# Block sums of the first MLP matrix, formed by adding transfers on GpSimd's queue instead of by VectorE

## The chip, the cores and the metric

The kernel runs on one core of a Trainium2 chip. The metric is device time in microseconds, from launch to end. Of the kernel before there are two timed runs, 1002.09 and 1002.58 us (median 1002.34), and one further execution that was profiled. Engines go by their profile names: PE (TensorE, with its weight loads shown as PEld), DVE (VectorE), ACT (ScalarE), POOL (GpSimd) and SP (SyncE, which here only issues transfers).

## The reference, cut to what matters

One layer of a hybrid decoder on 512 prompt tokens and 64 new tokens (576 columns in all). Two branches (RWKV-7 and attention) are merged to `m`; what the change touches is what follows:

```python
x = x + m @ lp['w_out']
hn = rmsnorm(x, lp['g_ffn'], NORM_EPS)
x = x + jnp.square(jax.nn.relu(hn @ lp['w_up'])) @ lp['w_down']
```

`w_out` is 1024 x 1024, `w_up` 1024 x 4096, `w_down` 4096 x 1024, all float32.

## The kernel before, in words

Everything is held transposed: channels on the 128 partitions, tokens in the free dimension. Every float32 operand of a large product is split in two: ACT copies it to a rounded `hi`, DVE subtracts to get `lo`, and PE multiplies hi·hi, hi·lo and lo·hi. So each weight tile that is loaded costs one ACT and one DVE instruction ("halving") before PE can use it.

**The output projection** (`dense(w_out[d], ...)`, called wo0, wo4, wo1, wo5, wo2, wo6, wo3, wo7 in this order) has 48 matmuls for each of its eight output tiles: two column halves of 288, 8 inner tiles, 3 products. Its weights come as two tiles of 4 inner blocks each (`raw_wo5_0` and `raw_wo5_4`, halved to `hi_wo5_0`/`lo_wo5_0` and `hi_wo5_1`/`lo_wo5_1`). Its result is taken from PSUM by DVE (`ya`, line 61), scaled on ACT to `hf`, and made at once into the seven blocks of the next product's moving operand (`h_b11`, `h_t1` and so on, by `put`).

**The first MLP matrix** is done with a seven-product scheme on 2 x 2 blocks in place of eight products. `up_pair(f1)` takes a pair of 128-row output tiles f1 and f1+1: the stationary blocks are a11, a12 (tile f1, first and second half of the inner dimension) and a21, a22 (tile f1+1). DVE forms four block sums of 128 x 512: s12 holds a21+a22 and a21+a22-a11, s34 holds a11-a21 and a12-(a21+a22-a11). Then s12, the tile of a11 and a12, s34 and a22 are halved, and seven products of 12 matmuls each run on PE in the order S1 (`uc`), A11 (`ua`), S2 (`ub`), A12 (`ua`), S3 (`ux`), S4 (`ud`), A22 (`ux`). There are 16 pairs. After a pair, four output tiles of the second matrix (`down`, `ps_dn`, 96 matmuls) run, except in the first and the last group of two pairs.

**Order.** A scheduler fixes each engine's order at build time from priorities (`prio`): loads of a job go first, halvings next, matmuls fill. On the chip every engine runs its row strictly in that order, and an instruction whose semaphore has not come stops all behind it on that engine, the transfer queues of SP and POOL included. Buffers are rings: `a` (the loaded rows of `w_up`) has 3 tiles of 512 KB, `s` 2, the halves `hi2`/`lo2` 3 each, and the ring of the other weights (`raw`, 256 KB) 3.

Of the kernel before, what the change touches and what calls it, by code (L numbers as in the profile page):

```python
# [8 lines left out]
F32 = mybir.dt.float32  # L9
F32R = mybir.dt.float32r  # L10
I32 = mybir.dt.int32
AF = mybir.ActivationFunctionType
# [3 lines left out]
P = 128  # L16
# [25 lines left out]
def tile_hybrid_step(ctx, tc, xT, xsT, ktab, vtab, s0T, ptab, w_in, vecs, w2a2, g2, lamv,  # L42
                     w_bra, w_brb, w_out, w_up, w_down, cst, bias_p, bias_s,
                     yT, kTo, vTo, Sp, Ss, sh):
    nc = tc.nc
# [9 lines left out]
    ring = {"job": 0}  # L55

    def act(out, in_, func=AF.Copy, **kw):
        ring["act"] = AE.activation(out=out, in_=in_, func=func, **kw)  # L58

    def tt(out, a, b, op, eng=None):  # L60
        ins = (eng or VE).tensor_tensor(out=out, in0=a, in1=b, op=op)  # L61
        if eng is None:
            ring["tt"] = ins

    def stt(out, a, s, b, op0, op1):
        VE.scalar_tensor_tensor(out=out, in0=a, scalar=s, in1=b, op0=op0, op1=op1)
# [16 lines left out]
    FEED, LATE, FILL = -1000000, 500000, 1000000  # L83

    @contextmanager
    def prio(at):
        was, tc.cur_priority = tc.cur_priority, at
        yield
        tc.cur_priority = was

    MUL, ADD, SUB, MAX = ALU.mult, ALU.add, ALU.subtract, ALU.max
# [20 lines left out]
    c = const.tile([P, C_END], F32, name="cst_sb")  # L112
# [158 lines left out]
    with tc.tile_pool(name="xin", bufs=2, reuse_waits="tile") as xin:  # L271
# [6 lines left out]
        for k in range(0, KT, 4):  # L278
            for j in range(3):
                with prio(FEED + 1000 + 10 * k + j):  # L280
                    name = f"raw_{'qkv'[j]}0_{k}"
                    if k == 0:
                        raw = ring["pool"].tile([P, 4, P], F32, tag="raw", name=name, bufs=3)
                    else:
                        raw = zw.tile([P, 1 + NX], F32, tag="z" if j else "tz", name=name,
                                      bufs=2 if j else 1)[:, :4 * P].rearrange("p (k w) -> p k w", k=4)
# [378 lines left out]
    for h in range(HB):  # L665
        if h:
            qkv(h)
        for cc in range(2):
            GE.tensor_copy(
                out=qbd[64 * cc:64 * cc + 64, :, h, 8 * cc:8 * cc + 8],  # L670
                in_=qT[64 * cc:64 * cc + 64, h, NPR:].rearrange("p (b q) -> p b q", b=NB))
# [448 lines left out]
    sp_ = pool("sp", 4, stack=ctx, reuse_waits="tile")  # L1120
# [6 lines left out]
    hfs = {}  # L1127
    for i, d in enumerate((0, 4, 1, 5, 2, 6, 3, 7)):
        xr = wt_.tile([P, NT], F32, tag="xr", name=f"xr{d}")
        with prio(FEED + 1000 * (ring["job"] + 1) - 1):  # L1130
            nc.sync.dma_start(out=xr, in_=xT[:, d])
        hf = hfs[d] = wt_.tile([P, NT], F32, tag="hf", name=f"hf{d}", bufs=3)
        k = d % 4

        def ev(ps, t0, n, d=d, k=k, xr=xr, hf=hf):
            x, h = ya[:, d, t0:t0 + n], hf[:, t0:t0 + n]
            tt(x, ps, xr[:, t0:t0 + n], ADD)
            act(h, x, scale=v(V_GF + d))
            if d < 4:
                if t0 == 0:  # L1140
                    put("b11", k, h)
                else:
                    t1 = wt_.tile([P, 288], F32, tag="t", name=f"t1_{k}", bufs=4)
                    tt(t1, h, hf[:, :288], SUB)
                    hfs["t1", k] = t1
                    put("t1", k, t1)
            elif t0:
                for n, x, y in (("t2", h, hfs["t1", k]), ("t3", h, hfs[k][:, 288:])):
                    t = hfs[n] = wt_.tile([P, 288], F32, tag="t", name=f"{n}_{k}", bufs=4)
                    tt(t, x, y, SUB)  # L1150
                    put(n, k, t)
                put("b22", k, h)
            else:
                put("b21", k, h)
                t4 = wt_.tile([P, 288], F32, tag="t", name=f"t4_{k}", bufs=4)
                tt(t4, h, hfs["t2"], SUB)
                put("t4", k, t4)
        dense(w_out[d], KT, mh, ml, HALF[::1 if d < 4 else -1], ev, f"wo{d}")

        for j, (t0, n) in enumerate(HALF):  # L1160
            o = acc[:, t0:t0 + n]
            if i == 0:
                act(o, ya[:, d, t0:t0 + n], AF.Square)
            else:
                sq = cbank(j, f"sq{d}{j}")[:, :n]
                act(sq, ya[:, d, t0:t0 + n], AF.Square)
                tt(o, o, sq, ADD)
# [12 lines left out]
    def up_pair(f1):  # L1180

        f2 = f1 + 1
        for f in (f1, f2):
            qs[f] = hq_pool.tile([P, 2, NT], F32R, tag="q", name=f"q{f}")
        with prio(FEED + 1000 * (ring["job"] + 1)):
            rows = [sp_.tile([P, 2, 4, P], F32, tag="raw", name=f"a{f}", bufs=3) for f in (f1, f2)]
            for r, f in zip(rows, (f1, f2)):
                nc.sync.dma_start(out=r.rearrange("p i k w -> p (i k) w"), in_=w_up[f])
        (a11, a12), (a21, a22) = ([r[:, i] for i in range(2)] for r in rows)
        s12, s34 = (sp_.tile([P, 2, 4, P], F32, tag="s", name=f"s{i}_{f1}", bufs=2) for i in (12, 34))  # L1190

        def halve(x, two, after):

            pl = sp_ if two else ring["pool"]
            shape = [P, 2, 4, P] if two else [P, 4, P]
            hi, lo = (pl.tile(shape, F32R, tag=t + "2" * two, name=f"{t}{after}_{f1}", bufs=3)
                      for t in ("hi", "lo"))
            with prio(FEED + 1000 * (ring["job"] + after) + 100):
                act(hi, x)
                tt(lo, x, f32(hi), SUB)  # L1200
            return [(hi[:, i], lo[:, i]) for i in range(2)] if two else (hi, lo)

        with prio(FEED + 1000 * (ring["job"] + 1) + 90):
            tt(s12[:, 0], a21, a22, ADD)
            tt(s12[:, 1], s12[:, 0], a11, SUB)
        S1, S2 = halve(s12, True, 1)
        A11, A12 = halve(rows[0], True, 2)
        with prio(FEED + 1000 * (ring["job"] + 3) + 90):
            tt(s34[:, 0], a11, a21, SUB)
            tt(s34[:, 1], a12, s12[:, 1], SUB)  # L1210
        S3, S4 = halve(s34, True, 5)
        A22 = halve(a22, False, 7)

        def e(n):
            return ft.tile([P, LAST[0][1]], F32, tag=n[0], name=f"{n}_{f1}", bufs=4 if n[0] == "c" else 1)[:, :288]

        def product(lhs, blk, ps, start, stop):
            job = ring["job"] = ring["job"] + 1
            i = 0
            skip = not (start and stop)  # L1220
            for k in range(4):
                for l, h in ((lhs[0], 0), (lhs[0], 1), (lhs[1], 0)):
                    with prio(FILL + 1000 * job + i):
                        ring["mm"] = PE.matmul(out=ps[:, :288], lhsT=l[:, k], rhs=hb[blk][:, h, k],  # L1224
                                               start=start and i == 0, stop=i == 11,
                                               skip_group_check=skip)
                    i += 1
            return prio(FEED + 1000 * job + 200)

        def out(f, half, c, r=None):  # L1230

            sp = slice(288 * half, 288 * half + 288)
            r = c if r is None else r
            act(r, c, AF.Relu)
            act(r, r, AF.Square)
            act(qs[f][:, 0, sp], r)
            tt(qs[f][:, 1, sp], r, f32(qs[f][:, 0, sp]), SUB)

        ba, bb, bc_, bx = (cbank(0, f"ua{f1}"), cbank(1, f"ub{f1}"), tbank(f"uc{f1}"), bank(f"ux{f1}"))
        product(S1, "t1", bc_, True, True)  # L1240
        with product(A11, "b11", ba, True, False):
            p1 = e("p1")
            act(p1, ba[:, :288])
        with product(S2, "t2", bb, True, True):
            u = e("u")
            tt(u, bb[:, :288], p1, ADD)
            w = e("w")
            tt(w, bc_[:, :288], u, ADD)
        with product(A12, "b21", ba, False, True):
            out(f1, 0, ba[:, :288], e("c11"))  # L1250
        with product(S3, "t3", bx, True, False):
            c22 = e("c22")
            tt(c22, bx[:, :288], w, ADD)
            out(f2, 1, c22)
        bd = cbank(1, f"ud{f1}")
        with product(S4, "b22", bd, True, True):
            c12 = e("c12")
            tt(c12, bd[:, :288], w, ADD)
            out(f1, 1, c12)
        with product(A22, "t4", bx, False, True):  # L1260
            c21 = e("c21")
            tt(c21, bx[:, :288], u, ADD)
            out(f2, 0, c21)
        ahead.append((ring["act"], ring["tt"]))
# [15 lines left out]
    for ch in range(8):  # L1280
        for i in range(2):
            up_pair(4 * ch + 2 * i)
            if ch == 0 and i == 0:
# [4 lines left out]
                with prio(FEED + 1000 * ring["job"]):  # L1288
                    m2 = stat.tile([P, 5], F32, tag="r", name="m2")
                    r2 = stat.tile([P, 5], F32, tag="s", name="r2")  # L1290
# [13 lines left out]
    rows = []  # L1304
    for d, n in enumerate((None, "t1", "b11", "t2", "b21", "t3", "b22", "t4")):
        if n:
            t = fp.tile([P, 2, 4, 288], F32R, tag=f"h_{n}", name=f"w3_{d}", bufs=1)
            t = t.rearrange("p i k t -> p (i k t)")
# [6 lines left out]
    for t0, n in LAST:  # L1315
# [55 lines left out]
        w = slice(0, len(tiles))  # L1371
# [133 lines left out]
```

## Time and profile before

| what | value |
|---|---|
| timed runs | 1002.09 and 1002.58 us, median 1002.34 |
| profiled execution, span from first to last instruction | 1004.0 us |
| PE busy | 975.5 us (97%) |
| DVE, ACT, POOL busy | 689.5, 497.3, 88.3 us |
| moved by DMA | 105.75 MB, mean 105 GB/s |

The profile gives the profiled execution's span and no other time of it; the span lies 1.7 us above the median of the timed runs, which were taken without the profiler. The page shows busy time by engine, the span in 40 slices, transfers by queue, the chain of work that ended last, and groups of instructions. Line numbers in its rows are those of the kernel before; line 58 is the helper for ACT, lines 61 and 66 those for two-input DVE instructions, line 72 the matmul helper, 1188 the loads of `w_up`, 1224 the matmuls of the seven products.

### The profile page before, as it was taken

The numbers are of one execution on the slowest core, as the hardware profiler recorded it, in microseconds if no ns is written. First come the engines' busy times: TensorE is split into PE (matmuls) and PEld (weight loads), VectorE is DVE, ScalarE is ACT, GpSimd is POOL, SyncE is SP. The second block draws the span as 40 slices with busy tenths as digits, with TensorE's granted clock in tenths as the row PEclk, the third lists the DMA queues.
The fourth block names the chain that finished last, engine by engine and source line by source line (L and its number), as shares of the span: only waits on it lengthen the run. The fifth ranks groups of instructions, "written<-read, shape, count | busy, mean of one in ns | idle before, by whom it ended". The sixth has DMA issues, their size and how long they took to land.

```text
span 1004.0 us, 24422 instructions
## 1 busy us (share of the span) xinstructions
PE 975.5 (97%) x10012; PEld 919.9 (92%) x10012; DVE 689.5 (69%) x1459; ACT 497.3 (50%) x1094; POOL 88.3 (9%) x171
## 2 busy tenths in 40 slices
PE   8999999899999999999999999999999999999996
PEld 8999998898887878888889999999999999999996
DVE  6698666774946669445588798966666666666744
ACT  6576555354435344443344666644444444444732
POOL 2511001301010340000300000000000000000001
PEclk9999999999989989999999999999999999999998
DMA  7312673121111225222377642222222222221402
GB/s 265 142 66 88 204 221 120 54 64 45 43 47 57 69 87 171 80 70 102 106 215 237 195 152 74 95 85 95 85 85 95 84 85 85 85 84 44 128 10 95
DMA packets 50833, 105.75 MB, mean 105 GB/s; under 512 B 6066, under 2 KB 8114, under 8 KB 50594
## 3 DMA queue, kind: packets, MB, share of 16 engines
q1 hardware_dynamic: 47442, 96.95, 30.2%
q0 software_dynamic: 1648, 5.35, 1.4%
q8 instruction: 79, 1.29, 0.5%
q10 hardware_dynamic: 1632, 1.89, 0.5%
q14 instruction: 32, 0.26, 0.1%
HBM read 89.38 MB, written 14.78 MB: 104 GB/s over the span
## 4 chain that ended last, share of the span: by engine, by line
PE 86%; DVE 6%; ACT 3%; DMA 2%; issue 2%; POOL 1%; SPq 0%; DVEq 0%; POOLq 0%; ACTq 0%
PE ps_dn L72 21%; PE ps_g L72 9%; PE ps_z L72 8%; PE ua L1224 5%; PE ux L1224 5%; PE ps_wo L72 4%; PE uc L1224 3%; PE ud L1224 3%; PE ub L1224 3%; PE ps_k L72 2%; PE ps_brb L72 2%; PE pch L72 2%; PE ps_q L72 2%; PE ps_v L72 2%; PE pA L72 2%
## 5 line engine op out<-in xcount | busy, mean ns | idle before, releaser
L72 PE MATMUL ps_dn<-q,hi_dn 128*128 128x288 f32 x768 | 154.7, 296 | 0.0
L72 PEld LDWEIGHTS ps_dn<-q,hi_dn 128*128 128x128 f32 x768 | 122.8, 188 | 1.5
L72 PE MATMUL ps_dn<-q,lo_dn 128*128 128x288 f32 x384 | 113.2, 295 | 0.0
L72 PE MATMUL ps_g<-xl,hi_g 128*128 128x288 f32 x256 | 80.2, 313 | 0.0
L72 PE MATMUL ps_g<-xh,lo_g 128*128 128x288 f32 x256 | 79.3, 310 | 0.0
L72 PE MATMUL ps_g<-xh,hi_g 128*128 128x288 f32 x256 | 79.2, 310 | 0.0
L72 PEld LDWEIGHTS ps_dn<-q,lo_dn 128*128 128x128 f32 x384 | 72.1, 188 | 0.0
L72 PE MATMUL ps_z<-xh,lo_z 128*128 128x288 f32 (+1 forms) x224 | 69.6, 311 | 0.0
L72 PE MATMUL ps_z<-xh,hi_z 128*128 128x288 f32 (+1 forms) x224 | 68.3, 305 | 0.0
L72 PE MATMUL ps_z<-xl,hi_z 128*128 128x288 f32 (+1 forms) x224 | 67.6, 302 | 0.0
L61 DVE TENSOR_TENSOR ya<-ya,ps_dn 128x288 f32<-128x288 f32 x96 | 43.4, 453 | 29.3 <-PE ps_dn L72 29.3
L58 ACT ACTIVATE hi_dn<-raw_dn 128x512 fp32r<-128x512 f32 x48 | 30.1, 628 | 57.0 <-PE ps_dn L72 57.0
L1224 PE MATMUL ua<-h_b,hi 128*128 128x288 f32 x256 | 53.2, 298 | 0.0
L1224 PE MATMUL ux<-h_t,hi 128*128 128x288 f32 x256 | 52.3, 296 | 0.0
L58 ACT ACTIVATE c<-c 128x288 f32<-128x288 f32 x112 | 48.4, 439 | 7.5 <-DVE c L61 5.8
L72 PEld LDWEIGHTS ps_g<-xh,hi_g 128*128 128x128 f32 x256 | 49.0, 191 | 2.9 <-issue 1.6
L72 PEld LDWEIGHTS ps_g<-xl,hi_g 128*128 128x128 f32 x256 | 49.0, 191 | 1.9
L72 PEld LDWEIGHTS ps_g<-xh,lo_g 128*128 128x128 f32 x256 | 49.1, 192 | 1.4
L58 ACT ACTIVATE hi<-a 128x1024 fp32r<-128x1024 f32 (+1 forms) x32 | 27.1, 846 | 42.0 <-PE ps_dn L72 34.3
L72 PE MATMUL ps_dn<-q,w 128*128 128x320 f32 (+1 forms) x336 | 46.4, 298 | 0.0
L61 DVE TENSOR_TENSOR lo<-s,hi 128x1024 fp32r<-128x1024 f32 x32 | 39.2, 1225 | 10.2 <-ACT hi L58 10.0
L72 PEld LDWEIGHTS ps_dn<-q,w 128*128 128x128 f32 x336 | 45.3, 190 | 0.1
(395 smaller groups left out, 2801.7 us busy)
## 6 DMA issues: line engine op xcount, KB each, us to landing
a<-in_w_up_dram SPq DMA_DIRECT2D x32, 512.0 KB, 3.3
raw_dn<-in_w_down_dram SPq DMA_DIRECT2D x64, 256.0 KB, 2.9
raw_g<-in_w_in_dram SPq DMA_DIRECT2D x32, 256.0 KB, 3.2
raw_z<-in_w_in_dram SPq DMA_DIRECT2D x28, 256.0 KB, 3.0
gt_d<-gg SPq DMA_DIRECT2D x16, 288.0 KB, 2.5
g<-gt_d SPq DMA_DIRECT2D x16, 288.0 KB, 3.7
kp<-in_ktab_dram SPq DMA_DIRECT2D x16, 256.0 KB, 4.0
vp<-in_vtab_dram SPq DMA_DIRECT2D x16, 256.0 KB, 3.7
```

What stands on the lines that cost most here:

```text
L58: ring["act"] = AE.activation(out=out, in_=in_, func=func, **kw)
L61: ins = (eng or VE).tensor_tensor(out=out, in0=a, in1=b, op=op)
L72: ring["mm"] = PE.matmul(out=out, lhsT=lhsT, rhs=rhs, start=start, stop=stop)
L1224: ring["mm"] = PE.matmul(out=ps[:, :288], lhsT=l[:, k], rhs=hb[blk][:, h, k], start=start and i == 0, stop=i == 11, skip_group_check=skip)
```

## The change

The second row tile of each pair enters with its sign turned, so that all four block sums are plain sums: s12 holds a21+a22 and a11+a21+a22, s34 holds a11+a21 and a12+a11+a21+a22. The signs are made good in three of the moving blocks (t1, t2 and t4 are formed negated, t2 and t4 by a `scalar_tensor_tensor`, one instruction as before) and in the Relu of the second tile, whose scale is -1.

The sums are no longer made by DVE. SP loads one addend into each half of the s tile (plain transfers), and POOL's queue then issues transfers from DRAM that add onto what lies in SBUF (`accum_op=ADD`): two for s12, three for s34. a1 and a22 are loaded by themselves. The ring of s12, a1 and s34 has 5 tiles of 512 KB; a22 comes from the 3-tile ring that the second matrix's weights use.

```diff
                     t1 = wt_.tile([P, 288], F32, tag="t", name=f"t1_{k}", bufs=4)
-                    tt(t1, h, hf[:, :288], SUB)
+                    tt(t1, hf[:, :288], h, SUB)
...
-                for n, x, y in (("t2", h, hfs["t1", k]), ("t3", h, hfs[k][:, 288:])):
+                for n in ("t2", "t3"):
                     t = hfs[n] = wt_.tile([P, 288], F32, tag="t", name=f"{n}_{k}", bufs=4)
-                    tt(t, x, y, SUB)
+                    if n == "t2":
+                        stt(t, h, -1.0, hfs["t1", k], MUL, SUB)
+                    else:
+                        tt(t, h, hfs[k][:, 288:], SUB)
...
-                tt(t4, h, hfs["t2"], SUB)
+                stt(t4, hfs["t2"], -1.0, h, MUL, SUB)
...
-            rows = [sp_.tile([P, 2, 4, P], F32, tag="raw", name=f"a{f}", bufs=3) for f in (f1, f2)]
-            for r, f in zip(rows, (f1, f2)):
-                nc.sync.dma_start(out=r.rearrange("p i k w -> p (i k) w"), in_=w_up[f])
-        (a11, a12), (a21, a22) = ([r[:, i] for i in range(2)] for r in rows)
-        s12, s34 = (sp_.tile([P, 2, 4, P], F32, tag="s", name=f"s{i}_{f1}", bufs=2) for i in (12, 34))
+            s12, a1, s34 = (sp_.tile([P, 2, 4, P], F32, tag="raw", name=f"{n}{f1}", bufs=5)
+                            for n in ("s12", "a1", "s34"))
+            a22 = ring["pool"].tile([P, 4, P], F32, tag="raw", name=f"a22{f1}", bufs=3)
+            r1, r2 = (w_up[f].rearrange("p (i k) w -> p i (k w)", i=2) for f in (f1, f2))
+            flat = lambda t: t.rearrange("p i k w -> p i (k w)")
+            twice = lambda r, i: r[:, i:i + 1].broadcast_to([P, 2, 4 * P])
+            nc.sync.dma_start(out=flat(s12)[:, 0], in_=r2[:, 0])
+            nc.sync.dma_start(out=flat(s12)[:, 1], in_=r1[:, 0])
+            nc.gpsimd.dma_start(out=flat(s12), in_=twice(r2, 1), accum_op=ADD)
+            nc.gpsimd.dma_start(out=flat(s12)[:, 1], in_=r2[:, 0], accum_op=ADD)
+            nc.sync.dma_start(out=flat(a1), in_=r1)
+            nc.sync.dma_start(out=flat(s34)[:, 0], in_=r2[:, 0])
+            nc.sync.dma_start(out=flat(s34)[:, 1], in_=r1[:, 1])
+            nc.gpsimd.dma_start(out=flat(s34), in_=twice(r1, 0), accum_op=ADD)
+            nc.gpsimd.dma_start(out=flat(s34)[:, 1:2], in_=r2[:, 0:1], accum_op=ADD)
+            nc.gpsimd.dma_start(out=flat(s34)[:, 1:2], in_=r2[:, 1:2], accum_op=ADD)
+            nc.sync.dma_start(out=a22.rearrange("p k w -> p (k w)"), in_=r2[:, 1])
...
-        with prio(FEED + 1000 * (ring["job"] + 1) + 90):
-            tt(s12[:, 0], a21, a22, ADD)
-            tt(s12[:, 1], s12[:, 0], a11, SUB)
         S1, S2 = halve(s12, True, 1)
-        A11, A12 = halve(rows[0], True, 2)
-        with prio(FEED + 1000 * (ring["job"] + 3) + 90):
-            tt(s34[:, 0], a11, a21, SUB)
-            tt(s34[:, 1], a12, s12[:, 1], SUB)
+        A11, A12 = halve(a1, True, 2)
         S3, S4 = halve(s34, True, 5)
...
-            act(r, c, AF.Relu)
+            act(r, c, AF.Relu, scale=-1.0 if f == f2 else 1.0)
```

Names in the changed program carry the pair's first tile number: `s120` and `s340` are s12 and s34 of the first pair (f1 = 0), `s122` and `s342` those of the second (f1 = 2).

On ACT, in the middle of the output projection, the kernel before has these rows (`hi1_0`, `hi2_0`, `hi5_0` are the halvings of s12, of the row tile and of s34 of the first pair):

```order
L58 ACTIVATE hi_wo5_0_8308<-raw_wo5_0_8304 128x512
L58 ACTIVATE hi1_0_8754<-s12_0_8750 128x1024
L58 ACTIVATE hf4_8131<-ya_8042,vec_73 128x288
L58 ACTIVATE hi2_0_8758<-a0_8746 128x1024
L58 ACTIVATE h_b21_8036<-hf4_8131 128x288
L58 ACTIVATE h_t4_8041<-t4_0_8210 128x288
L58 ACTIVATE sq40_8214<-ya_8042 128x288
L58 ACTIVATE hi_wo5_1_8312<-raw_wo5_4_8306 128x512
```

In the changed program the same stretch of ACT reads:

```order
L58 ACTIVATE h_b21_8036<-hf4_8131 128x288
L58 ACTIVATE hi1_0_8761<-s120_8746 128x1024
L58 ACTIVATE h_t4_8041<-t4_0_8210 128x288
L58 ACTIVATE hi2_0_8765<-a10_8747 128x1024
L58 ACTIVATE hi_wo5_1_8312<-raw_wo5_4_8306 128x512
```

The halving of s12 has moved back by three rows and stands behind `h_b21`, but still ahead of `hi_wo5_1`; it now waits for the adding transfers of its tile instead of for DVE. Eight rows further on, the changed ACT queue reads:

```order
L58 ACTIVATE h_t1_8038<-t1_1_8291 128x288
L58 ACTIVATE hi5_0_8769<-s340_8748 128x1024
L58 ACTIVATE hf5_8303<-ya_8042,vec_73 128x288
L58 ACTIVATE sq51_8389<-ya_8042 128x288
L58 ACTIVATE h_b22_8037<-hf5_8303 128x288
L58 ACTIVATE hi_wo2_1_8403<-raw_wo2_4_8397 128x512
```

The halving of s34 stood before `h_t1` and stands now behind it, still ahead of `hf5` and of `hi_wo2_1`, and waits for the three additions onto s34.

POOL's queue had nothing between the last store of the branches and the final norm; the changed program begins there with these rows (1197 and 1198 are the two adding transfers of s12, 1202 to 1204 the three of s34):

```order
L1197 DMA s120_8746<-in_w_up_dram 128x2x512
L1198 DMA s120_8746<-in_w_up_dram 128x512
L1202 DMA s340_8748<-in_w_up_dram 128x2x512
L1197 DMA s122_8939<-in_w_up_dram 128x2x512
L1203 DMA s340_8748<-in_w_up_dram 128x512
L1198 DMA s122_8939<-in_w_up_dram 128x512
L1204 DMA s340_8748<-in_w_up_dram 128x512
L1202 DMA s342_8941<-in_w_up_dram 128x2x512
```

All of them are new, and each addition onto a tile waits until the one before it on the same tile has landed, so that the queue stands still meanwhile.

On SP, at the same place, the difference is this (`xr` are the residual's input rows, `raw_wo` the projection's weights):

```order
 L1131 DMA xr4_8129<-in_xT_dram 128x576
-L1188 DMA a0_8746<-in_w_up_dram 128x1024
-L1188 DMA a1_8747<-in_w_up_dram 128x1024
+L1195 DMA s120_8746<-in_w_up_dram 128x512
+L1196 DMA s120_8746<-in_w_up_dram 128x512
+L1199 DMA a10_8747<-in_w_up_dram 128x1024
 L1131 DMA xr1_8220<-in_xT_dram 128x576
 L150 DMA raw_wo5_0_8304<-in_w_out_dram 128x512
 L150 DMA raw_wo5_4_8306<-in_w_out_dram 128x512
```

The two loads of whole row tiles have become three; behind the two loads of wo5 the changed queue goes on with s34 of the first pair and s12 and a1 of the second.

## The prediction

> **What bounds the kernel now.** I read the page first, then busy time by stretch, then PE's waits, then the chain that ended last.
>
> ```profile
> span 1004.0 us, 24422 instructions
> PE 975.5 (97%) x10012; PEld 919.9 (92%) x10012; DVE 689.5 (69%) x1459; ACT 497.3 (50%) x1094; POOL 88.3 (9%) x171
> ```
>
> PE is busy for 975.5 of 1004.0 us, so work taken from DVE can be worth at most what PE waits for DVE, in the stretches where the work stood. Those follow (columns: stretch and length, busy us of PE, PEld, DVE, ACT and POOL with instruction counts, granted clock, DMA share, GB/s).
>
> ```profile
> 556.00:568.00 12.00, 11.21 (x81) 10.52 (x80) 8.61 (x19) 7.68 (x17) 0.00 (x0) 1.00 0.74 246
> 568.00:604.00 36.00, 36.00 (x272) 36.00 (x273) 33.92 (x75) 26.24 (x58) 0.00 (x0) 1.00 0.50 151
> 604.00:645.00 41.00, 41.00 (x304) 39.99 (x304) 36.62 (x69) 27.95 (x65) 0.00 (x0) 1.00 0.24 78
> 645.00:941.00 296.00, 296.00 (x2216) 294.54 (x2215) 198.78 (x357) 141.46 (x265) 0.00 (x0) 1.00 0.26 84
> ```
>
> From 568 to 941 us PE never stops, at a granted clock of 1.00, though DVE is busy for 33.92 of 36 us in the projection. Only 556 to 568 us shows a gap, 12.00 - 11.21 = 0.79 us. PE's waits from 540 us on name it:
>
> ```profile
> PE ps_wo L72 <- DVE ya L61: 0.5, 1, 0.5
> PE ps_wo L72 <- DVE lo_wo L61: 0.2, 1, 0.2
> ...
> 558.70 0.40 PE L72 MATMUL ps_wo<-mh,hi_wo 128*128 128x288 f32 x1 [0.46 <-DVE ya L61]
> 562.79 0.69 DVE L61 TENSOR_TENSOR s<-a 128x512 f32<-128x512 f32 x1 [0.32 <-DMA a<-in_w_up_dram]
> ```
>
> The first stands at 558.70 us, before any block sum (the first of them begins at 562.79); only the second lies behind block sums. So the **gain is bounded by some 0.3 us** (the 0.79 less the 0.5).
>
> **What is taken away.** The four DVE groups that go:
>
> ```profile
> L61 DVE TENSOR_TENSOR s<-a x16: 684/687/697, 562.8 to 909.2; 128x512 f32<-128x512 f32 x16
> L61 DVE TENSOR_TENSOR s<-s,a x16: 681/684/685, 563.8 to 911.6; 128x512 f32<-128x512 f32 x16
> L61 DVE TENSOR_TENSOR s<-a,a x16: 644/685/693, 564.4 to 912.2; 128x512 f32<-128x512 f32 x16
> L61 DVE TENSOR_TENSOR s<-a,s x16: 678/684/693, 574.1 to 913.9; 128x512 f32<-128x512 f32 x16
> ...
> 564.97 0.45 DVE L61 TENSOR_TENSOR t<-hf,t 128x288 f32<-128x288 f32 x1
> 553.61 0.45 DVE L66 SCALAR_TENSOR_TENSOR ml<-g,mh 128x288 fp32r<-128x288 f32 x1
> ```
>
> 64 instructions of 0.685 us are 44 us of DVE, all beside a busy PE: worth 0.3 us as above. The signs cost nothing: t2 and t4, eight instructions in all, change from a form of 0.45 us to another of 0.45 us on the same two inputs, and the Relu's scale is a field of an instruction that is there already.
>
> **What is added: transfers.** Per pair SP issues six for two (1.75 MB for 1 MB), POOL five that add (1.75 MB). The issues themselves, 0.33 us each on SP and 0.55 us on POOL (rows below), fill 2 and 2.8 us of a period. Bandwidth over the 14 periods of the long stretch first. A period runs from one pair to the next:
>
> ```profile
> 750.50 1.60 PE uc L1224 x12
> ...
> 774.58 1.60 PE uc L1224 x12
> ...
> 798.67 1.60 PE uc L1224 x12
> ```
>
> It is 24.09 us and moves 2 MB now (a pair's 1 MB, four tiles of the second matrix at 256 KB), for the share of 0.26 above. After, 2.75 MB plain and 1.75 MB adding: 0.26 x 4.5/2 = 0.59 if an added byte costs as a plain one, 0.81 if twice, 1.04 if three times. So bandwidth binds only if adding costs nearly three times as much.
>
> **What is added: waits.** No row here shows a transfer that adds, so I bound it by plain ones (KB each, median us from issue to landing; then the loads' spread):
>
> ```profile
> a<-in_w_up_dram SPq DMA_DIRECT2D x32, 512.0 KB, 3.3
> raw_dn<-in_w_down_dram SPq DMA_DIRECT2D x64, 256.0 KB, 2.9
> ob_d<-obh POOLq DMA_DIRECT2D x4, 256.0 KB, 2.7
> out_kTo_dram<-kT POOLq DMA_DIRECT2D x4, 288.0 KB, 4.3
> ...
> DMA to landing us min/median/max: 3.1/3.3/7.2
> L1188 SPq DMA_DIRECT2D a<-in_w_up_dram x32: 327/328/430, 555.0 to 903.7; - x32
> 508.54 0.55 POOL L941 DMA_DIRECT2D out_Ss_dram<-s  x1 [1.08 <-DVE s L61]
> ```
>
> POOL's queue is about as quick as SP's (2.7 and 4.3 around 2.9). An addition cannot well land sooner than a load of its size: 3.3 us for the 512 KB ones (L1), 2.9 for the 256 KB ones (L2). It must also read what it adds to; if the two streams ran in series it would take twice that, 6.6 and 5.8. I take the middle, **L1 5.0, L2 4.4 us**, an estimate, and keep both ends. A tile's s34 chain is then L1 + 2 x L2 = 13.8 us (9.1 to 18.2).
>
> [...]
>
> *The long stretch.* ACT and DVE halve s12 of the next pair and, later, s34:
>
> ```profile
> 755.20 1.06 ACT L58 ACTIVATE hi<-s 128x1024 fp32r<-128x1024 f32 x1 [1.06 <-PE ub L1224]
> 760.35 1.04 ACT L58 ACTIVATE hi<-s 128x1024 fp32r<-128x1024 f32 x1
> ...
> 756.29 1.23 DVE L61 TENSOR_TENSOR lo<-s,hi 128x1024 fp32r<-128x1024 f32 x1
> ```
>
> This pair starts at 750.50 us. With five tiles in the ring, s34 of pair n takes the place of s12 of pair n-1, free when `lo` is done, at 757.5 us here, 7.0 us after the start of pair n-2. Its plain halves land 3.3 us later; it is halved 9.85 us after the start of pair n-1. The three additions therefore have 24.09 + 9.85 - 7.0 - 3.3 = 23.6 us. My 13.8 fits, and so does 18.2. s12 and a1 are freed a period earlier still; the loads of the second matrix queue behind a1, whose tile frees at the end of a pair, a full period ahead of their use. So here the cost is **zero**, with PE's 24.09 us as the cover.
>
> *The first pairs* (604 to 645 us, three pairs back to back) are tighter.
>
> ```profile
> 624.23 1.22 DVE L61 TENSOR_TENSOR lo<-s,hi 128x1024 fp32r<-128x1024 f32 x1
> ...
> 642.49 2.13 PE ps_dn L72 x16
> ```
>
> By the same count s34 of the fourth pair is loaded once s12 of the third is halved, at 625.5 us, and has its plain halves at 628.8. On the changed ACT it stands ahead of the halving of the third tile of the second matrix, which PE wants two tiles (2 x 3.2 us) after 642.5, with some 3 us of ACT and DVE work between: 646. That leaves 17 us for the additions; 13.8 still fits.
>
> *The projection* is where it does not fit. The rows:
>
> ```profile
> 555.58 7.19 DMA a<-in_w_up_dram
> ...
> 570.87 0.63 ACT L58 ACTIVATE hi_wo<-raw_wo 128x512 fp32r<-128x512 f32 x1 [0.79 <-PE ps_wo L72]
> 574.78 1.06 ACT L58 ACTIVATE hi<-s 128x1024 fp32r<-128x1024 f32 x1 [0.66 <-DVE s L61]
> ...
> 576.58 1.22 DVE L61 TENSOR_TENSOR lo<-s,hi 128x1024 fp32r<-128x1024 f32 x1
> 579.93 1.29 DVE L61 TENSOR_TENSOR lo_wo<-raw_wo,hi_wo 128x512 fp32r<-128x512 f32 x2
> ...
> 567.92 36.46 PE ps_wo L72 x273
> ```
>
> The two `w_up` loads take 7.2 us here, not 3.3, with the transfers at 246 GB/s, and land at 562.8 us; s12's plain half of these bytes lands at about 562.0. Then POOL: the first addition of s12 under the same load, 7.2 us, to 569.2; its second and, 0.6 us of issue later, the first of s34; then two more of s34, behind those of the second pair, which wait likewise. s12 is ready at 569.2 + 4.4 = 573.6, s34 at 569.2 + 0.6 + 13.8 = **583.6 us**. ACT reaches `hi5_0` (574.78 now) and waits; behind it stand `hf5`, `h_b22` and `hi_wo2_1`, and on DVE behind `lo5_0` the t blocks, `ya` of wo5 and `lo_wo2_1`. From the start of `hi` to the end of `lo_wo2_1` these take at least 1.1 (ACT) and 4.0 us (DVE, 576.58 to about 580.6): 588.7. PE needs that tile 16 matmuls into wo2; the chain's 273 matmuls take 36.46 us, 0.134 each, and the last 192 are wo2, wo6, wo3 and wo7, so wo2 starts at 604.38 - 25.6 = 578.7 and needs it at 580.9. The loss is 588.7 - 580.9 = **7.8 us**. The earlier wait of ACT on s12, ahead of `hi_wo5_1`, is contained in it, since the transfers run on while PE stands.
>
> SP waits too: s34 of the second pair wants the tile of s12, and behind it stand the loads of wo6; a1 of the third pair wants that of s34, free at 583.6 + 2.3 = 585.9, and behind it stand `xr6` and the loads of wo3.
>
> ```profile
> 580.68 4.78 SPq L150 DMA_DIRECT2D raw_wo<-in_w_out_dram  x3
> 590.18 0.62 ACT L58 ACTIVATE hi_wo<-raw_wo 128x512 fp32r<-128x512 f32 x1
> ```
>
> wo3, issued near 581 now and halved at 590.18, would be issued at 586.5, land near 590 and be halved 7.8 us later than now: covered. At the ends: with 9.1 us for the chain, and an unloaded first addition of 3.3, s34 is ready at 575.0 and the loss is nil; at 18.2, and 14.4 for the first, it is ready at 595.2, and the loss is 19.4, with some 2 us more in the first pairs.
>
> **Sum.** 7.8 - 0.3 = 7.5 us onto the profiled 1004.0 us. The timed median stands 1.7 us below that span; both move alike, so 1002.3 + 7.5 = 1009.8, say **1010 us**. That is 0.7%, within the 2% (20 us) that a measurement of this kernel can well tell from no change.
>
> **Rivals.** (1) *Hidden altogether*: additions land like plain loads, 1001.5 to 1004 us. For it speaks that POOL's stores land as fast as SP's loads; against it the second read, and the 0.74 share between 556 and 568 us. (2) *The chain of additions becomes the bound*: where L1 + 2 x L2 passes 23.6 us, 2.6 times the plain 9.1, every period waits on ACT at `hi5`, and lasts as long as the additions, with 14 periods. At three times (27.3 us) that is 14 x 3.7 = 52 us, and the projection loses 562.0 + 21.6 + 0.6 + 27.3 + 5.1 - 580.9 = 35.7: some 1090 us. For it speaks that nothing here shows how fast the adding path is; against it, that it takes 2.6 times the plain durations. (3) *In between*, the series end: 19.4 + 2 - 0.3, about 1023 us. [...]
>
> [...]
>
> **Chances.** Forecast (a few us lost in the projection, 1004 to 1014) 0.50; hidden 0.20; POOL held up 0.05; in between (up to 1030) 0.10; the chain as bound (beyond 1030) 0.15. Within 2% ends at 1022: forecast, hidden, held up, and 0.04 of the in-between case, less 0.01: 0.78. Slower by over 2% is the rest, 0.21; faster, which only an effect that I don't see could give, has the 0.01. The range goes from the hidden case's 1001 to 1030, which leaves out the 0.15.
>
> **What would show it.** Right: DVE busy some 44 us less; PE continuous from 645 us to the last products, period 24.09; one or two gaps of PE between 570 and 590 us, with ACT `hi` idle before it for some microseconds, released by an adding transfer; these landing in 4 to 7 us. Wrong: adding transfers at 8 us and more, ACT waiting for them in each period, a period over 24.09 us (then the time is 1030 and up); or no wait of ACT on them at all, and a time within 2 us of before.

## The result, and the profile after

The changed kernel takes 1034.6 us (1034.17 and 1035.02) against 1002.34 us: a ratio of 1.032 (95% interval 1.029 to 1.035), some 32 us slower. My 1010 us was too low, and the time lies above the upper end of 1030. The head of the page of the changed kernel:

```profile
span 1032.4 us, 24737 instructions
PE 979.7 (95%) x10012; PEld 922.8 (89%) x10012; DVE 654.2 (63%) x1395; ACT 497.1 (48%) x1094; POOL 169.0 (16%) x251
```

The span grew by 28.4 us, and DVE has its 64 instructions less. Busy time by stretch of the changed kernel (columns as before: PE, PEld, DVE, ACT, POOL, granted clock, DMA share, GB/s):

```profile
568.00:604.00 36.00, 23.24 (x137) 22.35 (x137) 17.17 (x35) 14.89 (x31) 10.50 (x11) 0.76 0.96 234
604.00:645.00 41.00, 39.95 (x298) 38.90 (x296) 32.83 (x69) 26.31 (x60) 4.26 (x4) 1.00 0.56 142
645.00:700.00 55.00, 45.02 (x317) 43.75 (x315) 28.31 (x52) 25.71 (x55) 13.32 (x13) 0.91 0.83 195
700.00:800.00 100.00, 100.00 (x749) 99.48 (x749) 57.75 (x104) 46.14 (x86) 20.50 (x21) 1.00 0.85 199
```

PE stands for 12.8 us in the projection, 1.0 us in the next stretch and 10.0 us around the fourth pair, together 23.8 us; from 700 us it never stops. PE's busy time grew by 4.2 us (979.7 for 975.5); its granted clock is below 1 in the two stretches with most of the gaps (0.76 and 0.91). PE's waits after 540 us, and from the chain that ended last the end of the projection and the long stretch's period:

```profile
PE ps_wo L72 <- DVE ya L61: 10.3, 3, 8.3
PE ps_dn L72 <- DVE ya L61: 9.5, 1, 9.5
PE ps_wo L72 <- ACT hi_wo L58: 3.5, 1, 3.5
...
609.00 11.14 PE ps_wo L72 x82
...
730.70 1.60 PE uc L1233 x12
754.78 1.59 PE uc L1233 x12
```

The projection ends at 620.14 us instead of 604.38, 15.8 us late; the rest of the 28.4 us is lost behind it. `hi_wo` stands behind a waiting halving on ACT, and `ya` behind that halving's `lo` on DVE. ACT's timeline shows where (the bracket is the idle time before a row and what released it), then DVE and PE at the fourth pair, then POOL's adding transfers (and, from the chain that ended last, the plain half of s34 of the fourth pair):

```profile
573.72 1.06 ACT L58 ACTIVATE hi<-s 128x1024 fp32r<-128x1024 f32 x1 [9.43 <-issue]
588.52 1.06 ACT L58 ACTIVATE hi<-s 128x1024 fp32r<-128x1024 f32 x1 [7.48 <-DMA s<-in_w_up_dram]
667.41 1.06 ACT L58 ACTIVATE hi<-s 128x1024 fp32r<-128x1024 f32 x1 [10.31 <-issue]
...
668.50 1.22 DVE L61 TENSOR_TENSOR lo<-s,hi 128x1024 fp32r<-128x1024 f32 x1 [10.07 <-ACT hi L58]
...
670.88 0.85 PE L72 MATMUL ps_dn<-q,hi_dn 128*128 128x288 f32 x2 [9.48 <-DVE ya L61]
...
557.32 1.26 POOL L1197 DMA_DIRECT2D s<-in_w_up_dram  x1 [52.07 <-DMA s<-in_w_up_dram]
567.45 0.93 POOL L1198 DMA_DIRECT2D s<-in_w_up_dram  x1 [8.88 <-DMA s<-in_w_up_dram]
568.40 1.21 POOL L1202 DMA_DIRECT2D s<-in_w_up_dram  x1
...
576.47 0.88 POOL L1203 DMA_DIRECT2D s<-in_w_up_dram  x1 [5.57 <-DMA s<-in_w_up_dram]
...
582.71 0.85 POOL L1204 DMA_DIRECT2D s<-in_w_up_dram  x1 [2.85 <-DMA s<-in_w_up_dram]
...
641.63 5.41 DMA s<-in_w_up_dram
...
647.61 1.20 POOL L1202 DMA_DIRECT2D s<-in_w_up_dram  x1 [1.02 <-DMA s<-in_w_up_dram]
...
655.31 0.88 POOL L1203 DMA_DIRECT2D s<-in_w_up_dram  x1 [3.88 <-DMA s<-in_w_up_dram]
...
662.71 0.86 POOL L1204 DMA_DIRECT2D s<-in_w_up_dram  x1 [1.50 <-DMA s<-in_w_up_dram]
```

Three halvings wait long: s12 and s34 of the first pair (ready at 573.7 and 588.5), and s34 of the fourth pair (667.4). For the first and the third the profile names no releaser ("issue"); by time it is the landing of the last addition, issued at 567.45 and at 662.71. Behind each stands work that PE needs. Each step of a chain starts when the one before has landed, and that takes 6 to 10 us here, not 4.4 to 7.2. All landings of the first addition onto s12 (line 1197) and onto s34 (1202), 512 KB each, and of the last one (1204), 256 KB:

```profile
L1197 POOL DMA_DIRECT2D s<-in_w_up_dram x16: 1188/1197/1517, 557.3 to 912.5; - x16
DMA to landing us min/median/max: 7.2/10.3/11.7
...
L1202 POOL DMA_DIRECT2D s<-in_w_up_dram x16: 1203/1203/1460, 568.4 to 934.2; - x16
DMA to landing us min/median/max: 5.4/8.0/9.5
...
L1204 POOL DMA_DIRECT2D s<-in_w_up_dram x16: 852/859/909, 582.7 to 943.9; - x16
DMA to landing us min/median/max: 3.7/4.9/7.4
```

### The profile page after: what moved, and what is told of

Read it like the earlier page. It is cut to its first block, busy times and chain, and to the rows that moved or that the text cites. A ratio compares the mean times of both kernels' runs of the same rounds, so it can differ in the third digit from the quotient of the medians.

```text
span 1032.4 us, 24737 instructions
## 1 busy us (share of the span) xinstructions
PE 979.7 (95%) x10012; PEld 922.8 (89%) x10012; DVE 654.2 (63%) x1395; ACT 497.1 (48%) x1094; POOL 169.0 (16%) x251
## 4 chain that ended last, share of the span: by engine, by line
PE 77%; DVE 7%; DMA 5%; issue 4%; ACT 4%; POOL 2%; SPq 0%; DVEq 0%; POOLq 0%; ACTq 0%
PE ps_dn L72 20%; PE ps_g L72 9%; PE ps_z L72 8%; PE ua L1233 4%; PE ux L1233 4%; DMA s<-in_w_up_dram 3%; PE ps_k L72 2%; PE uc L1233 2%; PE ud L1233 2%; PE ub L1233 2%; PE ps_brb L72 2%; PE pch L72 2%; PE ps_q L72 2%; PE ps_v L72 2%; PE pA L72 2%
## 5 line engine op out<-in xcount | busy, mean ns | idle before, releaser
L58 ACT ACTIVATE hi<-s 128x1024 fp32r<-128x1024 f32 x32 | 33.7, 1053 | 44.5 <-issue 19.7
L72 PE MATMUL ps_wo<-mh,hi_wo 128*128 128x288 f32 x128 | 40.4, 315 | 13.9 <-DVE ya L61 10.3
```

The source lines that it names most:

```text
L72: ring["mm"] = PE.matmul(out=out, lhsT=lhsT, rhs=rhs, start=start, stop=stop)
```

## The experiments

My theory after the result (A, then made more exact as F): a chain of additions in series takes as long as its bytes need on the shared DMA engines; where the tile is released too late for it, or where other work stands behind the waiting halving on ACT, PE stops. The rivals: queue and waits alone (B), the engines taken away from the projection's own loads (C), the long stretch paying too (D). Ratios are against the kernel before on the same chip.

| run | what it is | ratio (95% interval) |
|---|---|---|
| e8_dve_all | all loads and signs of the change, sums on VectorE | 1.001 (1.000 to 1.003) |
| e1_plain | copying in place of adding | 1.021 (1.018 to 1.025) |
| e2_late | halvings of the first pair placed later | 1.020 (1.017 to 1.022) |
| e5_own_tile | one tile more for s34 | 1.025 (1.023 to 1.026) |
| e6_late_own | both | 1.011 (1.009 to 1.013) |
| e14_plain_late_own | both, copying | 1.003 (1.001 to 1.004) |
| e9_tiny | additions of 16 columns | 1.006 (1.005 to 1.008) |
| e13_tiny_late | the same, halvings later | 1.000 (0.999 to 1.001) |
| e3_dve_first4 | four pairs on VectorE | 1.021 (1.019 to 1.023) |
| e15_long_own0 | the same, a22 of the first pair early | 1.013 (1.011 to 1.015) |
| e11_long_only | the same, one tile more | 1.003 (1.001 to 1.004) |
| e7_one_add | one addition a tile | 1.090 (1.087 to 1.092) |
| e12_one_add_placed | the same, sums placed later | 1.001 (1.000 to 1.003) |

**What is not the additions.** VectorE adds in place; all else is the change's, but that a22 is loaded ahead of a1 (that of the first pair into the ring of s12).

```diff
-nc.gpsimd.dma_start(out=flat(s12), in_=twice(r2, 1), accum_op=ADD)   # and the other four
+tt(s12[:, 0], s12[:, 0], a22, ADD)
+tt(s12[:, 1], s12[:, 1], s12[:, 0], ADD)
+tt(s34[:, 0], s34[:, 0], a1[:, 0], ADD)
+tt(s34[:, 1], s34[:, 1], s12[:, 1], ADD)
```

> No adding transfer at all: the same plain loads into the same tiles as in the changed kernel, the same signs, and VectorE adds in place (a22 of the first pair lies in the ring of s12, so that it can be loaded early). It prices what of the change is left beside the additions. All theories: 0 to 2 us above the kernel before; were it 5 us or more, the rings and the six loads for two would bear part of the loss.

1.4 us above (0 to 2.8): six loads for two, the rings and the signs bear next to nothing.

**The price alone.**

```diff
+tt(zf[:, :, 0], src[:, :2], src[:, :2], ADD)      # ties it to the pair
+nc.gpsimd.dma_start(out=zf, in_=r1)
+nc.gpsimd.dma_start(out=zf, in_=r1, accum_op=ADD)
+nc.gpsimd.dma_start(out=zf, in_=r2[:, 1:2].broadcast_to([P, 2, 4 * P]), accum_op=ADD)
+nc.gpsimd.dma_start(out=zf[:, 1], in_=r2[:, 0])
+nc.gpsimd.dma_start(out=zf[:, 1], in_=r2[:, 0], accum_op=ADD)
```

> The kernel before, with five transfers more in each of ten pairs on GpSimd's otherwise empty queue, one after the other onto a scratch tile that nothing reads: plain 512 KB, adding 512 KB, adding 512 KB with the source read twice, plain 256 KB, adding 256 KB. It measures the price where the DMA share is about 0.3. Theory A: plain ones 3 to 3.5 us, adding 512 KB 6 to 8 us, adding 256 KB 3.7 to 5. Rival E (an addition alone is as quick as a copy and only the crowd of the changed kernel slows it): 3.3 to 4 us for all 512 KB ones. The time stays at 1002 to 1004 us in both.

The landings of its five transfers, in the order of the diff:

```profile
DMA to landing us min/median/max: 3.4/4.1/4.6
...
DMA to landing us min/median/max: 5.0/5.3/6.7
...
DMA to landing us min/median/max: 5.4/6.0/8.4
...
DMA to landing us min/median/max: 2.8/2.9/3.3
...
DMA to landing us min/median/max: 3.5/3.6/4.2
```

With no other addition under way (DMA share 0.66 from 700 to 800 us, for 0.85 in the changed kernel), an addition of 512 KB lands in 5.3 us (6.0 with the source read twice) for 4.1 of a copy, one of 256 KB in 3.6 for 2.9: a fourth to a half more, where I had expected 6 to 8 and 3.7 to 5. That lies between theory A and rival E. So my 5.0 was close for an addition alone, and 4.4 was too long; the 8 to 10 us come with the load of the changed kernel. Its time, 1007.57 us in one run beside 999.64, was not the expected 1002 to 1004: VectorE's own small instruction, which ties the transfers to the pair, waited for the scratch tile, and PE shows a gap of 2.8 us behind it; the rest stays open.

**Copying in place of adding.**

```diff
-nc.gpsimd.dma_start(out=flat(s12), in_=twice(r2, 1), accum_op=ADD)   # all five
+nc.gpsimd.dma_start(out=flat(s12), in_=twice(r2, 1))
```

> The five transfers of each pair on GpSimd's queue copy instead of adding (the block sums are left out); bytes, queues, rings, waits and the order on every engine are those of the changed kernel. Theory A (an adding transfer takes the DMA engines about twice the time of a plain one, and the loss comes from that): DMA share of the long stretch falls from 0.82-0.85 to about 0.6 (0.26 x 4.5/2), the 512 KB transfers land in 3.5 to 5 us instead of 8 to 10, the gap of PE between 660 and 671 us goes, those between 568 and 592 us shrink to 3 us or less: 1002 to 1007 us. Rival B (the waits in GpSimd's in-order queue and the bytes, whatever the transfers do): the gaps stay, 1028 to 1036 us.

Neither came: 21 us above the kernel before, between both. The three gaps stay and are smaller. PE's waits in it, and the share of the queues (packets, MB, share of 16 engines over the span): before, changed, copying.

```profile
PE ps_wo L72 <- DVE ya L61: 8.5, 3, 6.7
PE ps_dn L72 <- DVE ya L61: 6.0, 1, 6.0
...
q0 software_dynamic: 1648, 5.35, 1.4%
...
q0 software_dynamic: 17264, 34.71, 18.1%
...
q0 software_dynamic: 10096, 34.71, 10.1%
```

Less what the queue carries in the kernel before, the same 29.4 MB take 16.7% of 1032.4 us when they add and 8.7% of 1022.4 us when they copy: **1.94 times the engine time**. The long stretch has a DMA share of 0.85 with adding, where I had 0.81 for an added byte at twice the cost. But two thirds of the loss stay without any adding: long series, with more bytes, in the wrong places.

**The two places.**

```diff
+at = {1: ("wo2", 1), 5: ("wo3", 1)}.get(after) if f1 == 0 else None
+with tc.issue_after(ring[at].ins) if at else nullcontext():    # hi of wo2_1, wo3_1
     act(hi, x)
```

> The changed kernel, but in the first pair the halving of s12 stands on ACT behind the second halving of wo2 and that of s34 behind the second of wo3, so that nothing of the projection is queued behind them; the adding transfers are the same. Theory A with the place I predicted (ACT's in-order queue turns late sums into a PE gap): the 14 us of gaps in the projection and the slowed clock behind them go but for 1 to 3 us, the gap of the fourth pair (9.5 us and a slowed clock behind it) stays: 1012 to 1018 us. Rival C (the adding transfers take the DMA engines away from the projection's own weight loads): PE still waits 5 us or more for halved wo tiles, 1020 us and up.

```diff
+sx_ = pool("sx", 1, stack=ctx, reuse_waits="tile")
+own = f1 >= 6 and f1 % 4 == 2          # s34 of these pairs in sx_, not in the ring of five
```

> The changed kernel, with one tile of 512 KB more that s34 of every second pair uses, from the fourth pair on: its loads and additions no longer wait for the halving of the pair before. Theory F (a chain of transfers in series takes some 20 to 26 us from its plain load to its last addition; the long stretch leaves it 27 us, the fourth pair 16 to 20 us, since its tile comes free late): the gap of the fourth pair goes, that of the projection stays: 13 to 20 us above the kernel before. Rival G (the transfers themselves are behind, so that the next pair waits in its place): a gap of 6 us or more stays between 655 and 700 us, 25 us and more above.

> Both repairs: the first pair's halvings behind those of wo2 and wo3, and the further tile for s34 of every second pair from the fourth on. All adding transfers stay. Theory F: the two repairs add up, 3 to 9 us above the kernel before (what is left are the shared DMA engines during the projection). Rival G: 15 us and more above, with a gap after the third pair.

PE's largest wait after 540 us, of the late halvings, of the further tile, and of both:

```profile
PE ps_dn L72 <- DVE ya L61: 8.4, 1, 8.4
...
PE ps_wo L72 <- DVE ya L61: 8.9, 3, 7.5
...
PE ux L1239 <- ACT hi L58: 2.5, 1, 2.5
```

Each repair takes away its own gap and leaves the other, and they add up: some 12 us of the 32 (1.032 to 1.020) and 7 us (to 1.025), both together 21 us. Rival G falls: from 655 to 700 us the kernel with the further tile has 1.6 us of waits. Rival C is not the main cause, since with the late halvings PE waits only 1.9 us in all for halved wo tiles (its time does lie at the edge of C's 1020 us). The times are up to 5 us above those expected, since with both repairs 11 us are left, in small gaps before 645 us and a slower clock behind them. Is that the adding?

> Both repairs of the order (late halvings of the first pair, a further tile for s34 of every second pair from the fourth on) with copying in place of adding (sums left out). With adding it stood 11 us above the kernel before. Theory F: what is left there is the adding itself, which keeps the DMA engines twice as long during the first three pairs: 1 to 6 us above. Rival K (the extra loads and the rings): 9 us and more above, as with adding.

Yes: with copies instead, 2.5 us are left, so 8.7 of the 11 us are the adding itself, and rival K falls. This much of rival C remains: the additions keep the DMA engines busier at the start. Busy time by stretch, with adding (DMA share 0.90), then copying (0.74):

```profile
604.00:645.00 41.00, 36.90 (x250) 34.64 (x249) 26.82 (x51) 23.35 (x55) 10.26 (x10) 0.94 0.90 204
...
604.00:645.00 41.00, 41.00 (x304) 39.93 (x303) 31.89 (x60) 27.99 (x63) 8.01 (x13) 1.00 0.74 254
```

**Bytes or waits.** Each adding transfer cut to 16 columns, then that with the late halvings:

```diff
-nc.gpsimd.dma_start(out=flat(s12), in_=twice(r2, 1), accum_op=ADD)
+nc.gpsimd.dma_start(out=flat(s12)[:, :, :16], in_=twice(r2, 1)[:, :, :16], accum_op=ADD)   # and so the others
```

> The changed kernel with each adding transfer cut to 16 of its 512 columns (the sums of the other columns are left out): queues, rings, waits, series and the order on every engine stay, the adding bytes go (1.75 MB to 0.05 MB a pair). Theory F (series of transfers, each as long as its bytes on shared engines take): steps of some 2 us, a chain of 6 to 8 us, the gap of the fourth pair gone, at most 3 us of gaps in the projection: 0 to 5 us above the kernel before. Rival B (waiting in GpSimd's queue and order alone costs it): 15 us and more above.

> The kernel with adding transfers of 16 columns (sums left out) together with the late halvings of the first pair. Without the late halvings it stood 6.3 us above the kernel before, with one gap of 6.6 us before PE's wo matmuls. Theory F (that gap is the series of small transfers ahead of the halving of s34, at some 2.6 to 3.9 us each, in front of a halved wo tile on ACT): the gap goes, 0 to 3 us above the kernel before. Rival K (it comes from the loads behind the rings on SP's queue): 5 us and more above.

```profile
s<-in_w_up_dram POOLq DMA_DIRECT2D x48, 8.0 KB, 2.6
s<-in_w_up_dram POOLq DMA_DIRECT2D x32, 16.0 KB, 3.9
...
PE ps_wo L72 <- DVE ya L61: 7.0, 2, 6.6
```

A step of 8 KB still takes 2.6 us and one of 16 KB 3.9, so that s34 waits for 3.9 + 2 x 2.6 = 9.1 us even with hardly any bytes; the fourth pair stands this, the projection does not, until the halvings are placed later: then the time is that of the kernel before. The 6.3 us was a little over my 5, and its gap was that of ACT's order; rival K falls here too.

**The long stretch and the first pair that adds.**

```diff
+dve = f1 < 8            # VectorE's sums in four pairs, the rest as in the changed kernel
```

> In the first four pairs the adding transfers are replaced by four VectorE additions in place on the same tiles and the same plain loads; the other twelve pairs add by transfer as in the changed kernel. Theory A (lost only at the start, nothing in the long stretch): no gap of PE from 568 us to the last products, 1002 to 1004 us. Rival D (the long stretch pays too, with its DMA share of 0.85): 1006 us and up, with gaps after 700 us.

The theory as it stood then was wrong: 21 us above. One gap was my edit's (a22 of the first pair is loaded last, and PE waits for its halvings, 6.5 us); the other, 7.3 us, stands at 672 to 680 us, at the fifth pair. With a22 early, and then with the further tile for the fifth and each second pair after it:

> VectorE makes the sums of the first four pairs, the other twelve add by transfer, all in the ring of five tiles (no further tile). With the further tile it stood 2.9 us above the kernel before and had no gap. Theory F (whichever pair adds first finds too short a lead, since its tile is released by the halving of the pair before, which itself waits for its sums): a gap of 5 to 9 us between 660 and 690 us, 8 to 12 us above. Rival L (the further tile did nothing; only the first four pairs matter): no gap, 0 to 4 us above.

> VectorE makes the sums of the first four pairs (as in the kernel without adding transfers), the other twelve pairs add by transfer, and s34 of the fifth, seventh, ... pair has the further tile. Theory F (adding costs nothing where the lead is long enough): no gap of PE from 568 us on beyond 1 us, 0 to 4 us above the kernel before. Rival D (the long stretch pays for a DMA share of 0.85): 6 us and more above.

13 us above without the further tile, a little over the 8 to 12. ACT's wait in that kernel between 600 and 700 us, and then PE's:

```profile
ACT hi L58 <- DMA s<-in_w_up_dram: 6.8, 1, 6.8
...
PE ps_dn L72 <- DVE ya L61: 7.2, 2, 6.8
```

With it there is neither, and the time is 2.9 us (1.3 to 4.4) above the kernel before, with twelve of sixteen pairs adding; 1.4 us of that the loads and rings cost without any addition. So the gap belongs to the first pair behind the quick start that adds, whichever that is, for want of a tile released early enough; in the long stretch itself PE shows no wait, and rivals D and L fall.

**How near the long stretch is.**

```diff
 nc.gpsimd.dma_start(out=flat(s34)[:, 1:2], in_=r2[:, 1:2], accum_op=ADD)
+nc.gpsimd.dma_start(out=flat(s34)[:, 1:2], in_=r2[:, 0:1], accum_op=ADD)
+nc.gpsimd.dma_start(out=flat(s34)[:, 1:2], in_=r2[:, 1:2], accum_op=ADD)
```

> The changed kernel with the last two additions onto s34 made twice (five in series, 2.25 MB adding a pair; the sum holds two addends twice). Theory F with the lead read from the changed kernel's trace (from the release of the tile to its halving 27.0 us in the long stretch, of which 24.3 are used): two more steps of some 5 us make 35 us, 8 us over the lead, so each period grows to about 30 to 33 us and ACT waits for an addition in each: 80 to 120 us above the changed kernel. Rival I (the engines' share is the bound: 0.85 x 5/4.5 = 0.94 is still under 1): the period stays 24.1 us, no more than 15 us above.

1100.64 us in one run, some 68 us above the changed kernel (1.032 x 1000.56), not 80 to 120. The chain that ended last shows every second pair; the first and the last of four:

```profile
784.99 1.59 PE uc L1235 x12
...
956.39 1.60 PE uc L1235 x12
```

(956.39 - 784.99) / 6 = 28.6 us for 24.1: the period lengthens as theory F has it, by 4.5 us and not by 8. Rival I falls. So the rival in which the chain becomes the bound was at most two steps away: with three additions, 24.3 of the 27.0 us between the release of the tile and its halving are used. By these numbers one further step of some 5 us would already be too many; no run shows that.

**One addition a tile.**

```diff
-nc.gpsimd.dma_start(out=flat(s12), in_=twice(r2, 1), accum_op=ADD)
-nc.gpsimd.dma_start(out=flat(s12)[:, 1], in_=r2[:, 0], accum_op=ADD)
+nc.gpsimd.dma_start(out=flat(s12)[:, 0], in_=r2[:, 1], accum_op=ADD)
+tt(s12[:, 1], s12[:, 1], s12[:, 0], ADD)        # s34 likewise: + a11, then + s12[:, 1]
```

> One addition of 256 KB per tile in place of two and three: GpSimd's queue adds a22 onto the first half of s12 and a11 onto the first half of s34, VectorE makes the second halves (two of its four sums, in place). No addition waits for another on the same tile. Theory F (the series is what is late): no gap beyond the first microseconds, 0 to 4 us above the kernel before. Rival H (any addition ahead of the first pair's halvings is late): gaps of 5 us or more between 565 and 592 us, 8 us and more above.

The worst miss: 0 to 4 us were expected, 89 measured, with 0.5 MB of adding bytes a pair in place of 1.75. DVE's timeline in the long stretch:

```profile
749.47 0.69 DVE L61 TENSOR_TENSOR s<-s 128x512 f32<-128x512 f32 x1 [4.08 <-issue]
750.08 0.45 DVE L61 TENSOR_TENSOR q<-c,q 128x288 fp32r<-128x288 f32 x1
```

VectorE's sum onto s12, whose halving comes much later, stands ahead of `q` and `ya`, and waits 4.1 to 5.0 us in each of the three periods from 700 to 800 us (for its addition, by time: POOL issues that at 742.80, and they land in 5.8 us there). Part of the 89 us is PE's slower clock behind these gaps: the granted clock is 0.91 from 700 to 800 us, and 1.00 there in the next kernel. That is the same kernel with VectorE's two sums placed later, the one onto s12 behind the `u` of the pair before:

```diff
+with tc.issue_after((ring["u"] if f1 else ring["wo2", 1]).ins):      # s34 likewise: c12, wo3
     tt(s12[:, 1], s12[:, 1], s12[:, 0], ADD)
```

> The kernel with one addition of 256 KB a tile once more; VectorE's sum onto s12 now stands behind the making of u in the pair before, that onto s34 behind its c12, and those of the first pair behind the second lo of wo2 and wo3. Transfers, bytes and rings stay as they were. Theory F (what took 89 us there was the place of a waiting instruction in VectorE's in-order queue, 4 to 5 us in each period): the period is 24.1 us again, 0 to 5 us above the kernel before. Rival J (the additions or their bytes took it): 60 us and more above.

1.1 us above (-0.4 to 2.7): the 89 us were the places of VectorE's sums in an in-order queue, and rival J falls. Rival H's gaps of 5 us before 592 us had not come: PE's longest wait between 560 and 604 us was 2.4 us. No version beats the kernel before; PE is busy for 97% of it, and nothing here gives PE less to do.

## Why the prediction was wrong

- *The gain is bounded by 0.3 us* held: with all four sums of a pair on VectorE (e8) and with two (e12) the time is the same within 1.5 us, and no version is faster.
- *The places* held: gaps of PE in the projection, ACT's `hi` before them waiting for adding transfers, and "tighter" first pairs.
- *The long stretch costs zero* held: period 24.08 us, share 0.85 between my 0.81 and 1.04. The margin was thin, 2.7 us: the medians of the three steps add up to 18.4 us (8.0, 5.5, 4.9), already past the 18.2 that I had as the upper end.
- **L1 5.0 and L2 4.4 us failed**, and with them the ends: I bounded one addition by one plain load, with 6.6 and 5.8 at the upper end. Alone they measure 5.3 to 6.0 and 3.6; in the changed kernel 8.0 to 10.3 and about 5, since the additions crowd each other (DMA share 0.85 in the long stretch, for 0.66 in e4) and hold the engines for 1.94 times the time of copies. I had reckoned the engines' share for the long stretch alone; in the projection it is 0.96. The first pair's measured steps, in my own formula, give the right loss: s34 ready at 588.5, plus 5.1, less 580.9, is 12.7 us, and PE stood 12.8 us there in its two gaps, where I had 7.8. The formula leaves out the slower clock, and the loads of wo, which I had as covered (ACT waits 2.6 us for one, and PE then 0.9 us more); the projection as a whole ends 15.8 us late.
- **"That leaves 17 us for the additions; 13.8 still fits" failed**: s34 of the fourth pair took 667.4 - 647.0 = 20.4 us for them, and its plain halves 5.4 us, not 3.3. The 17 us were too many as well: I let PE run two output tiles of the second matrix before it needed anything, but it stops after one (24 matmuls), because the `ya` that frees its PSUM tile stands on DVE behind the `lo` of the waiting halving. I had priced the upper end of this at 2 us; it was 9.5 us of gap, without which the time would be some 1025 us, inside the range. Since even copies leave 6.0 us here, what was mis-sized was the series under load more than the adding.
- **A term was missing**: PE ran slower behind each of the three gaps (granted clock 0.50 for 4 to 6 us after it had work again), 2 to 3 us a gap by the estimate in the last section. Over the whole span the busy time grew by 4.2 us only, since at 568 us the profiled execution of the changed kernel stood some 30 matmuls (4 us) ahead of that of the kernel before.
- The rivals: hidden altogether falls; POOL held up, given 0.05, is shown by no run (the issue of an adding transfer of 512 KB, its source read once, took 844 to 902 ns in e4, with DVE busy for 65.59 of the 100 us from 700 us on); the in-between case with its 1023 us was nearest in kind, given 0.10 and sized too small. The time lies in the band of the chain as bound (beyond 1030 us), but that mechanism did not come: the period did not grow. Of the signs of being wrong only the first came, additions of 8 us and more.

## What to carry to other kernels

A chain of dependent transfers is sized by its steps under the load that it makes itself (here 8.0 to 10.3 us for an addition of 512 KB that took 5.3 to 6.0 alone), and set against the time from the release of its buffer to its use at the tightest place, which here is the start, not the steady stretch. What cost the time here was less the waiting than what stood behind it on an engine that runs in order: moving the instruction that waits and giving its tile an earlier release gave back two thirds (21 of 32 us). And moving block sums off DVE, for which PE had waited some 0.3 us at most, gained nothing here, though DVE was busy for 69% of the span.

## What the runs showed of the hardware that I had not expected

An adding transfer took 1.94 times the engine time of a copy of the same bytes (16.7% of 1032.4 us for 8.7% of 1022.4 us), but alone it landed only a fourth to a half later (5.3 and 6.0 us for 4.1, 3.6 for 2.9); the queue's packets for the same bytes grew from 10096 to 17264. Small transfers did not get short: 2.6 us for 8 KB, 3.9 us for 16 KB.

PE's granted clock fell 2 to 4 us after PE stopped in each of the three gaps. Stretches of 2 us of the changed kernel, around the first gap and behind the last:

```profile
572.00:574.00 2.00, 0.00 (x0) 0.00 (x0) 0.00 (x0) 0.28 (x1) 0.00 (x0) 0.66 1.12 204
574.00:576.00 2.00, 0.00 (x0) 0.00 (x0) 1.19 (x2) 2.00 (x4) 0.00 (x0) 0.50 1.10 200
...
672.00:674.00 2.00, 2.00 (x10) 2.00 (x10) 1.46 (x4) 0.74 (x2) 0.00 (x0) 0.50 1.04 300
674.00:676.00 2.00, 2.00 (x13) 2.00 (x13) 0.45 (x1) 0.00 (x0) 0.86 (x1) 0.74 0.99 298
```

The last matmul before the first gap starts at 568.36 us, and the clock falls at about 572.6, 4 us later; in the second gap, before which the last one starts at 587.46, it falls after 2 us already (0.67 from 589 to 591 us); in the third, before which the last one starts at 661.10, it falls at about 664.8, nearly 4 us later. It is back at 1.00 some 4 us after PE has work again at 670.88 us, and 6 us after 576.91 (0.78 from 582 to 584). So each of these gaps cost 2 to 3 us more than its length, an estimate: half of the 4 to 6 us at a granted clock of 0.50.
